# Three sums of a recurrence-and-convolution loop moved from VectorE to GpSimd, with more convolution steps in each round

## The chip, the cores and the metric

The kernel runs on one core of a Trainium2 chip. The metric is the time of one execution on the device, in microseconds. The engines are TensorE (PE: matmuls; PEld: its weight loads), VectorE (DVE), ScalarE (ACT), GpSimd (POOL) and SyncE (SP, which issues most DMAs). Each has its own queue of instructions and works through it in order; waits between engines are semaphores.

## What is computed

A two-layer backbone over 1024 latent tokens with 1024 channels and 256 context tokens. The even layer, where the change lies, projects the modulated tokens by one matrix and splits the result into five parts:

```python
va, vg, ga, xb, gb = jnp.split(z, [W_CONV, 2 * W_CONV, 3 * W_CONV, 3 * W_CONV + W_LRU], axis=-1)
y_a = conformer_conv(va, vg, p) * jax.nn.silu(ga)
y_b, hT = rglru_branch(xb, p, h0, True)
y_b = y_b * jax.nn.silu(gb)
return jnp.concatenate([y_a, y_b], axis=-1) @ p["w_out"], hT
```

`conformer_conv` gates `va * sigmoid(vg)`, runs a depthwise convolution of 31 taps along the tokens, and a layer norm over the channels. `rglru_branch` runs a short convolution of 4 taps, four gate products for each head, and a linear recurrence `h = a * h + b` along the tokens in both directions, first over the context and then over the latent tokens; `y = hs[:, :, 0] + hs[::-1, :, 1]` adds the two directions. The odd layer is a pooling mixer with two large projections; a final RMS norm ends it.

## The kernel before

**Tiling.** Channels lie on the 128 partitions, tokens along the columns. There are `KT = 8` blocks of 128 channels; a block of 1024 tokens is worked in two halves of `H = 512` columns. Every product is made of three matmuls, high part by high part, high by low and low by high (`mm3_fixed`, line 682). A weight is therefore loaded raw, its high part is cast on ACT, and its low part is the difference, by `gp` on POOL (`raw_split`, 701).

**An order written by hand.** In this part each engine's instructions are chained in the order of the program text: `on` (666) makes each instruction follow the last one of its engine. `act`, `cast`, `gp` and `vec` put instructions on ACT, ACT, POOL and DVE. So an instruction whose input is late holds up all that stands behind it on the same engine. DMAs issued by `nc.sync` are queued on SP.

**The rounds** are the loop over `j` from 903 on, one for each block of channels. Round `j` does, on PE, the products `vg` (48 matmuls), `va` (48), the context part of the next block `xbc` (24 narrow ones; not in the last round, where `gb0` takes the place of the next `xb`), and then the gate products `g` of this block, interleaved with `xb` of the next. Around them stand:

- the short convolution of block `j` on ACT and DVE (`first_tap`, `other_taps`; tile `uc`) and its split (`uh`, `ul`);
- the recurrence of block `j-1`, called `state`: `rec_input` and `rec_scaled` multiply on POOL (tiles `l`), `rec_tanh`, `rec_exp` and `rec_root` work on ACT, `rec_scan` (863) does on DVE for each direction a scaling of 1280 columns and two scans (256 and 1024 columns), and `rec_sum` (877) adds the two directions, 1024 columns, and stores the sum by SP into a DRAM buffer, `yb_raw`;
- `raw_split` of the next weights: `va`, `xb`, the gates', and in the midst of the gate products that of the next round's first weight (`vg`, or `gb` after the last round). PE reads this one at the start of the next round. On POOL it stands behind `rec_scaled`;
- the long convolution. `conv(j)` (734) is a generator of 49 steps on DVE, 50 for the last three blocks, most of them one `scalar_tensor_tensor` over some 505 columns from SBUF into an accumulator in PSUM. `fill(n)` (809) makes the next `n` steps. In rounds 1 to 7 there are 32 steps: 2 and 3 about the short convolution, 2 ahead of `ul`, 10 and 6 in `va`, 3 ahead of the context part, 6 at the end. Round 0 makes 22.

The convolution works on even and odd tokens apart (two phases) and needs, besides them, the sum of the two phases. For the first five blocks (`NSPREAD`) this sum is made ahead of its use by `spread_sum` (790) into one half of the tile `cL`; later blocks make it in a step of the convolution. `edge_sum` (786) is a product over 8 columns that goes with it. `ln_sums` (779) adds each block whose convolution has ended to two running sums, `lnsum`, one for each half, from which the layer norm's mean is made later. `at_rest` (801) calls both at the end of a round's scans, and once more after the rounds.

**The tail.** After the rounds come the products `gb1` to `gb7` and the eight of `wob` on PE. Into the stretch of `gb1` to `gb3` fall the recurrence of the last block, with `fill(2)` and `fill(24)` ahead of its `rec_scan`; then `rec_sum` and `at_rest` (1062, 1063). Then `gated` (1219) loads `yb_raw` back (tile `yr`), multiplies it on DVE by the SiLU of `gb` (tile `sb`), casts the result on ACT (`ybh`) and takes its low part on POOL (`ybl`), with a few convolution steps between; the splits of `gb5` to `gb7` and of the `wob` weights stand in the same queues. The tiles that `gated` writes lie where tiles of the rounds lay, so it waits for the last reader of those. In the `wob` products the convolutions are ended, seven steps to a half product, and the sums and the mean of the layer norm stand at a fixed place (1324).

Of the kernel before, what the change touches and what calls it, by code (L numbers as in the profile page):

```python
# [17 lines left out]
C = 256  # L18
# [3 lines left out]
H = 512  # L22
HALF = (slice(0, H), slice(H, S))
# [28 lines left out]
def body(ctx, tc, xT, ctxT, cc, ccol, modT, modW, win, gw, wout, wu, grp, wg, wo1, small, edge, ident, outT):  # L52
    nc = tc.nc
    mult, add, sub = ALU.mult, ALU.add, ALU.subtract
# [25 lines left out]
    def atile(name):  # L80
        return apool.tile([P, NR * PW], F32, tag="acc", name=name)
# [5 lines left out]
    def wide(name):  # L87
        return pc.tile([P, S], F32, tag="xb", name=name)
# [67 lines left out]
    def mm3_steps(ps, w, xs, cols, ks=KT, mm=nc.tensor.matmul):  # L156
        hi, lo = w
        xh, xl = xs
        for k in range(ks):
            kc = slice(k * P, (k + 1) * P)  # L160
            mm(ps, hi[:, kc], xh[k][:, cols], start=(k == 0), stop=False)  # L161
            mm(ps, hi[:, kc], xl[k][:, cols], start=False, stop=False)
            mm(ps, lo[:, kc], xh[k][:, cols], start=False, stop=(k == ks - 1))
            yield
# [9 lines left out]
    def col(o, n=1):  # L174
        return sm[:, o : o + n]
# [120 lines left out]
    cL = cpool.tile([P, D], F32, name="cL")  # L296
    with ExitStack() as sctx:
# [325 lines left out]
        first = (x for h in range(2) for x in mm3_steps(xb0[:, HALF[h]], ws[8], (hh, hl), HALF[h], KT, mm))  # L623
# [42 lines left out]
    def on(eng, f, *args, **kw):  # L666
        with ExitStack() as octx:
            if eng in last:
                octx.enter_context(tc.issue_after(last[eng].ins))
            last[eng] = f(*args, **kw)  # L670
        return last[eng]
# [7 lines left out]
    def gp(*args, **kw):  # L679
        return on("pool", nc.gpsimd.tensor_tensor, *args, **kw)  # L680
# [11 lines left out]
    def all_of(steps):  # L692
        for _ in steps:
            pass
# [16 lines left out]
    us = []  # L711
# [6 lines left out]
    lnacc = [atile("lnsum0"), atile("lnsum1")]  # L718
    fixed = [True]

    def vec(f, **kw):
        return on("vec", f, **kw) if fixed[0] else f(**kw)
# [53 lines left out]
    ended, summed, spread_ = [0], [1], [0]  # L776
    NSPREAD = 5

    def ln_sums():
        for j in range(summed[0], ended[0]):  # L780
            for h in range(2):
                first = us[0][:, HALF[h]] if j == 1 else lnacc[h][:, :H]
                vec(nc.vector.tensor_tensor, out=lnacc[h][:, :H], in0=first, in1=us[j][:, HALF[h]], op=add)
        summed[0] = max(summed[0], ended[0])

    def edge_sum(j):
        vec(nc.vector.scalar_tensor_tensor, out=edge_junk, in0=us[j][:, 1::2][:, H - 8 :], scalar=-1.0,
            in1=taps[:, j, 0:16:2], op0=mult, op1=mult, accum_out=edges[:, j : j + 1])

    def spread_sum():  # L790
        j = spread_[0]
        edge_sum(j)
        vec(nc.vector.tensor_tensor, out=cL[:, HALF[j % 2]], in0=us[j][:, 1::2], in1=us[j][:, 0::2], op=add)
        spread_[0] += 1

    def both_sum(j):
        while spread_[0] <= j:
            spread_sum()
        return cL[:, HALF[j % 2]]

    def at_rest():
        ln_sums()
        while spread_[0] < min(whole_[0], ended[0] + 2, NSPREAD):
            spread_sum()


    going, begun, whole_ = [iter(())], [0], [0]
# [1 line left out]
    def fill(n):  # L809
        while n > 0:  # L810
            try:
                next(going[0])
                n -= 1
            except StopIteration:
                if begun[0] >= whole_[0]:
                    return
                going[0] = conv(begun[0])
                begun[0] += 1

    with ExitStack() as actx:  # L820
# [42 lines left out]
        def rec_scan(st, d):  # L863
            at, iu = st[2][2 * d : 2 * d + 2]
            vec(nc.vector.scalar_tensor_tensor, out=iu, in0=at, scalar=1.0, in1=iu, op0=add, op1=mult)
            if d == 0:
                ctx_, lat = slice(0, C), slice(C, E)
                first = iu[:, C - 1 : C]
            else:
                ctx_, lat = slice(C - 1, None, -1), slice(E - 1, C - 1, -1)  # L870
                first = iu[:, 0:1]
            vec(nc.vector.tensor_tensor_scan, out=iu[:, ctx_], data0=at[:, ctx_], data1=iu[:, ctx_],
                initial=0.0, op0=mult, op1=add)
            vec(nc.vector.tensor_tensor_scan, out=iu[:, lat], data0=at[:, lat], data1=iu[:, lat],
                initial=first, op0=mult, op1=add)

        def rec_sum(st):
            hs, hb = st[2][1], st[2][3]
            vec(nc.vector.tensor_tensor, out=hs[:, C:], in0=hs[:, C:], in1=hb[:, C:], op=add)
            nc.sync.dma_start(yb_raw[st[0]], hs[:, C:])  # L880


# [19 lines left out]
        state, free = None, [L[0], L[1], L[2], L[3], L[4], L[5]]  # L902
        for j in range(KT):
# [66 lines left out]
            if state is None:  # L970
                for m in range(3 * KT - 2, 3 * KT):
                    gate_dot(m, gate_raw[m - 2 * KT])
                vec(nc.vector.tensor_tensor, out=m0[:, 0, 2 * KT :], in0=m0[:, 0, 2 * KT :],
                    in1=col(O_MB + 2 * KT, KT), op=add)
# [13 lines left out]
            if state is not None:  # L988
                for d in range(2):
                    rec_scan(state, d)  # L990
                rec_sum(state)
            at_rest()
            xb = wide(name if final else f"xb{j + 1}")
            steps = (x for h in range(2) for x in mm3_fixed(xb[:, HALF[h]], wnext, (hh, hl), HALF[h]))
            if state is None:
# [11 lines left out]
                    w = raw_split(raw, name)  # L1007
                    rec_input(now, 0)
            all_of(steps)
            fill(19 if state is None else 6)  # L1010
            state, uc = now, ucn


# [46 lines left out]
        gws[4] = hi, lo  # L1060
        rec_scan(state, 1)
        rec_sum(state)
        at_rest()

    cpool.release()
# [172 lines left out]
    for j in range(3, KT + 1):  # L1238
        if j == 4:
            gb_weights(j + 2)  # L1240
        if j < KT:
            gb_silu(j)
        if 4 < j < KT - 1:
            gb_weights(j + 2)
        if 3 < j < KT - 2:
            gb_product(j + 2, gws[j + 2])
        gated(j - 1, (0, 0, 4, 5, 5, 3, 1, 0)[j - 1])
        if j == KT:
            gb_weights(KT + 1)
            fill(8)  # L1250
        ln_sums()
# [62 lines left out]
    for m in range(KT):  # L1314
# [7 lines left out]
        for h in range(2):  # L1322
            all_of(steps[h])
            if (m, h) == (KT - 2, 0):
                while ended[0] < KT:
                    fill(1)
                ln_sums()
                for q, parts in enumerate([mean_parts(lnacc[q][:, :H], f"mu{q}") for q in range(2)]):
                    ln_mean(q, parts)
            elif m >= KT - 2:  # L1330
                q = m - KT + 2
                for j in range(KT) if (m, h) != (KT - 1, 1) else ():
                    ln_square(j, q)
                    if j > 1:
                        ln_add(j - 2, q)
                if (m, h) != (KT - 1, 1):
                    for j in (KT - 2, KT - 1):
                        ln_add(j, q)
                    lnparts = mean_parts(lnacc[0][:, :H], "ln0") if q == 0 else lnparts
                else:  # L1340
                    ln_root(0, lnparts)
                    lnparts = mean_parts(lnacc[1][:, :H], "ln1")
            wob_evict(m, h)
            fill(7)
            ln_sums()
# [988 lines left out]
```

## Time and profile before

| | |
|---|---|
| median of 3 runs | 1267.16 us (1267.01 to 1267.77) |
| span of the profiled execution, first to last instruction | 1263.6 us |
| what the median has beyond that span | 3.6 us |
| ACT, share of the span | 653.8 us (52%) |
| rounds 1 to 7 | 119 to 414 us from the span's start |
| gb and wob products after the rounds | 414 to 579 us |

The 3.6 us are the launch and the end, which lie outside the span; the profiled execution's own time is read as its span and these. In the lines below, `L670` is the helper `on`, so almost all instructions of this part have that one line, and they are told apart by their tiles: `l<-l,l` with 128x1280 on DVE is a scaling of the recurrence, with 128x1024 on DVE the sum of the two directions, on POOL with 128x1280 a product of the recurrence; `lnsum` is a sum for the layer norm, `cL<-u` the sum of the two phases, `wl_...` the low part of a weight. A line of a timeline gives the start and the length in us, the engine, what is written and read, how many instructions were merged (x3), and in brackets how long the engine had been idle and what ended that.

### The profile page before, as it was taken

What the parts mean: (1) busy time and instruction counts of PE and PEld (TensorE: products, weight loads), DVE (VectorE), ACT (ScalarE), POOL (GpSimd) and SP (SyncE); (2) the same over time, 40 slices, a digit from 0 to 9 for tenths busy, and PEclk for the clock granted to TensorE, in tenths of its full rate; (3) what the DMA queues carried; (4) which work ended last, traced back from release to release, by engine and by line L of the source; (5) the groups of instructions that cost most, each with busy time, mean ns of one, the idle gap of its engine ahead of it and who ended that gap; (6) DMA issues with size and microseconds to landing.
All of it is one profiled execution on the core that took longest, in us unless ns stands there. A gap on an engine that the chain in (4) does not pass through costs nothing.

```text
span 1263.6 us, 16209 instructions
## 1 busy us (share of the span) xinstructions
PE 1249.8 (99%) x5866; PEld 1035.6 (82%) x5866; DVE 1139.3 (90%) x1746; ACT 653.8 (52%) x952; POOL 295.7 (23%) x176
## 2 busy tenths in 40 slices
PE   9999999999999999999999999999999999999997
PEld 7788888888888888888887878888888888888786
DVE  7799999999999999998978969999899987977975
ACT  8464566656666534237535445744343444644642
POOL 0015364436444547543210023000000000000002
PEclk9999999999999999999999999999999999999999
DMA  9970121112121233442436666344323334759723
GB/s 376 388 254 33 52 65 46 63 43 75 42 84 42 84 119 132 159 150 84 147 112 225 202 206 183 103 136 148 125 94 140 117 125 126 268 199 335 285 71 134
DMA packets 78705, 182.29 MB, mean 144 GB/s; under 512 B 7712, under 2 KB 23328, under 8 KB 78624
## 3 DMA queue, kind: packets, MB, share of 16 engines
q1 hardware_dynamic: 67328, 172.33, 39.8%
q10 hardware_dynamic: 11296, 8.92, 2.2%
q8 instruction: 46, 0.75, 0.2%
q14 instruction: 35, 0.29, 0.1%
HBM read 137.18 MB, written 44.04 MB: 143 GB/s over the span
## 4 chain that ended last, share of the span: by engine, by line
PE 70%; DVE 18%; DMA 7%; issue 2%; ACT 2%; POOL 1%; SPq 0%; POOLq 0%; ACTq 0%; DVEq 0%
PE wob L670 7%; DVE conv L670 5%; PE va L670 5%; PE xb L670 4%; PE vg L670 4%; DVE l L670 3%; PE fold L670 3%; PE g L670 3%; PE qb_v L1153 2%; PE ga L670 2%; PE qb_g L1156 2%; PE ga L161 2%; PE qb_v L1156 2%; PE qb_g L1155 2%; PE qb_g L1153 2%
## 5 line engine op out<-in xcount | busy, mean ns | idle before, releaser
L670 DVE SCALAR_TENSOR_TENSOR conv<-u,sm,conv 128x505 f32<-128x505 f32 (+6 forms) x224 | 153.6, 744 | 1.0
L2045 POOL TENSOR_TENSOR o<-x,rr 128x256 f32<-128x256 f32 (+1 forms) x10 | 9.2, 952 | 448.4 <-ACT rr L2045 448.4
L670 ACT ACTIVATE l<-g,sm 128x512 f32<-128x512 f32 (+1 forms) x96 | 58.7, 619 | 57.7 <-PE g L670 57.0
L670 POOL TENSOR_TENSOR l<-l,l 128x1280 f32<-128x1280 f32 x16 | 47.1, 2967 | 25.6 <-ACT l L670 15.1
L670 PE MATMUL gb<-h0h,wl_gb 128*128 128x512 f32 x128 | 49.9, 390 | 0.4 <-POOL wl_gb L670 0.4
L670 PE MATMUL va<-h0h,wl_va 128*128 128x512 f32 x128 | 49.9, 390 | 0.2 <-DVE wl_va L670 0.2
L98 ACT CAST wq_g<-wr_g 128x512 fp32r<-128x512 f32 x48 | 28.2, 621 | 41.9 <-DMA wr_g<-wg 15.6
L670 PE MATMUL gb<-h0l,wh_gb 128*128 128x512 f32 x128 | 49.8, 389 | 0.0
L670 PE MATMUL gb<-h0h,wh_gb 128*128 128x512 f32 x128 | 49.8, 389 | 0.0
L670 PE MATMUL va<-h0l,wh_va 128*128 128x512 f32 x128 | 49.8, 389 | 0.0
L670 PE MATMUL va<-h0h,wh_va 128*128 128x512 f32 x128 | 49.8, 389 | 0.0
L670 PE MATMUL wob<-ybl,wh_wob 128*128 128x512 f32 x128 | 49.8, 389 | 0.0
L670 PE MATMUL wob<-ybh,wl_wob 128*128 128x512 f32 x128 | 49.8, 389 | 0.0
L670 PE MATMUL wob<-ybh,wh_wob 128*128 128x512 f32 x128 | 49.8, 389 | 0.0
L670 DVE TENSOR_TENSOR_SCAN l<-l,l 128x256 f32<-128x256 f32 (+1 forms) x32 | 48.7, 1521 | 1.1
L670 DVE SCALAR_TENSOR_TENSOR conv<-cL,wsum,conv 128x506 f32<-128x506 f32 (+3 forms) x70 | 48.1, 745 | 0.2
L670 POOL TENSOR_TENSOR l<-l,uc 128x1280 f32<-128x1280 f32 x16 | 47.6, 2999 | 0.0
L98 ACT CAST wq_wo<-wr_wo 128x512 fp32r<-128x512 f32 x48 | 28.6, 620 | 35.5 <-DVE wr_wo L1134 12.4
L98 ACT CAST wq_v<-wr_v 128x512 fp32r<-128x512 f32 x48 | 28.1, 620 | 33.7 <-DMA wr_v<-wfold 16.6
L670 PE MATMUL xb<-h0l,wh_xb 128*128 128x512 f32 x112 | 43.8, 391 | 0.0
L670 PE MATMUL xb<-h0h,wh_xb 128*128 128x512 f32 x112 | 43.8, 391 | 0.0
L670 POOL TENSOR_TENSOR wl_xb<-wr_xb,wh_xb 128x1024 fp32r<-128x1024 f32 x7 | 16.8, 2407 | 114.5 <-ACT wh_xb L670 114.5
(680 smaller groups left out, 4362.5 us busy)
## 6 DMA issues: line engine op xcount, KB each, us to landing
modw<-modW SPq DMA_DIRECT2D x16, 512.0 KB, 10.2
mod<-modT SPq DMA_DIRECT2D x32, 256.0 KB, 3.4
wr_v<-wfold SPq DMA_DIRECT2D x16, 512.0 KB, 4.0
wr_g<-wg SPq DMA_DIRECT2D x16, 512.0 KB, 4.3
wr_wo<-wo SPq DMA_DIRECT2D x16, 512.0 KB, 4.1
mod<-modT SPq DMA_DIRECT2D x14, 512.0 KB, 4.5
y_b<-y SPq DMA_DIRECT2D x24, 256.0 KB, 3.5
y_t<-y SPq DMA_DIRECT2D x24, 256.0 KB, 3.1
```

The lines of the kernel that those rows point to most:

```text
L98: return (nc.scalar.copy(hi, src), eng.tensor_tensor(out=lo, in0=src, in1=hi.bitcast(F32), op=sub))
L161: mm(ps, hi[:, kc], xh[k][:, cols], start=(k == 0), stop=False)
L670: last[eng] = f(*args, **kw)
L1153: nc.tensor.matmul(ps, hi, xh[k], start=(first and k == 0), stop=False, skip_group_check=not first)
L1155: nc.tensor.matmul(ps, hi, xl[k], start=False, stop=False, skip_group_check=not first)
L1156: mm = nc.tensor.matmul(ps, lo, xh[k], start=False, stop=(k == KH - 1), skip_group_check=not first)
L2045: tail[eng] = f(*args, **kw)
```

## The change

`ln_sums`, `spread_sum` and `rec_sum` put their additions on GpSimd through `gp` where they are called in the rounds and by `at_rest`; calls of `ln_sums` elsewhere, `both_sum`'s call of `spread_sum` and all of `edge_sum` stay on DVE. In the rounds `at_rest` now comes ahead of `rec_sum`, so that on POOL the layer norm's and the phases' sums are queued before the sum of the two directions; after the rounds the order stays as it was. The last `fill` of rounds 1 to 7 makes 10 steps instead of 6. The number of all steps stays the same, so later fills find fewer left.

```diff
+    def plus(eng, **kw):
+        (gp if eng == "pool" else lambda **k: vec(nc.vector.tensor_tensor, **k))(**kw)
+
-    def ln_sums():
+    def ln_sums(eng="vec"):
         for j in range(summed[0], ended[0]):
             for h in range(2):
                 first = us[0][:, HALF[h]] if j == 1 else lnacc[h][:, :H]
-                vec(nc.vector.tensor_tensor, out=lnacc[h][:, :H], in0=first, in1=us[j][:, HALF[h]], op=add)
+                plus(eng, out=lnacc[h][:, :H], in0=first, in1=us[j][:, HALF[h]], op=add)
         summed[0] = max(summed[0], ended[0])
...
-    def spread_sum():
+    def spread_sum(eng="vec"):
         j = spread_[0]
         edge_sum(j)
-        vec(nc.vector.tensor_tensor, out=cL[:, HALF[j % 2]], in0=us[j][:, 1::2], in1=us[j][:, 0::2], op=add)
+        plus(eng, out=cL[:, HALF[j % 2]], in0=us[j][:, 1::2], in1=us[j][:, 0::2], op=add)
         spread_[0] += 1
...
     def at_rest():
-        ln_sums()
+        ln_sums("pool")
         while spread_[0] < min(whole_[0], ended[0] + 2, NSPREAD):
-            spread_sum()
+            spread_sum("pool")
...
         def rec_sum(st):
             hs, hb = st[2][1], st[2][3]
-            vec(nc.vector.tensor_tensor, out=hs[:, C:], in0=hs[:, C:], in1=hb[:, C:], op=add)
+            gp(out=hs[:, C:], in0=hs[:, C:], in1=hb[:, C:], op=add)
             nc.sync.dma_start(yb_raw[st[0]], hs[:, C:])
...
                 for d in range(2):
                     rec_scan(state, d)
+            at_rest()
+            if state is not None:
                 rec_sum(state)
-            at_rest()
...
             all_of(steps)
-            fill(19 if state is None else 6)
+            fill(19 if state is None else 10)
             state, uc = now, ucn
```

By the program text, counted in steps, the layer norm pairs of the changed kernel fall into rounds 3, 4, 6 and 7 and into the tail (before: 3, 5, 6 and the tail), the phase sums made by `at_rest` into rounds 0 to 4 (before: 0 to 3 and 5). Between the scans of round 7 and those of the last block lie 36 steps (before: 32).

## Prediction

> **What bounds the kernel now.** I read the page's engine table first, then the chain that ended last, PE's timeline, and the table of waits on PE.
>
> ```profile
> PE 1249.8 (99%) x5866; PEld 1035.6 (82%) x5866; DVE 1139.3 (90%) x1746; ACT 653.8 (52%) x952; POOL 295.7 (23%) x176
> ```
> ```profile
> 246.64 10.88 PE vg L670 x48
> ...
> 289.12 10.88 PE vg L670 x48
> ```
> ```profile
> 331.44 0.39 PE L670 MATMUL vg<-h0h,wh_vg 128*128 128x512 f32 x1
> 331.67 0.39 PE L670 MATMUL vg<-h0l,wh_vg 128*128 128x512 f32 x1
> 331.89 0.39 PE L670 MATMUL vg<-h0h,wl_vg 128*128 128x512 f32 x1
> ```
> ```profile
> PE gb L670 <- POOL wl_gb L670: 0.4, 1, 0.4
> ```
>
> A matmul is shown as 0.39 us long, but the next one starts 0.23 us later (331.44, 331.67, 331.89): they overlap, and the distance of their starts is PE's pace. Forty-eight of them take 10.88 us in the chain, the same 0.227 us each. Round 5 begins 42.48 us after round 4 (289.12 - 246.64), and the chain between the two is all PE. So in the rounds PE never stands still: lighter work on DVE, busy as it is at 90%, shortens nothing there by itself. Between the rounds and the wob products PE waits once, 0.4 us, for a weight's low part from POOL. What the change can gain near its own place is that fraction of a microsecond; what it can lose is any new wait that reaches PE. A difference under 0.2% (2.5 us) cannot be told from no change in this kernel.
>
> **The change part by part.** DVE's rows at the end of round 5, after the scans of round 7, and in the tail:
>
> ```profile
> 314.45 1.52 DVE L670 SCALAR_TENSOR_TENSOR uc<-xbc,sm,uc 128x254 f32<-128x254 f32 x3 [0.68 <-ACT uc L670]
> 315.88 1.48 DVE L670 SCALAR_TENSOR_TENSOR l<-l,l 128x1280 f32<-128x1280 f32 x1
> ...
> 325.00 1.23 DVE L670 TENSOR_TENSOR l<-l,l 128x1024 f32<-128x1024 f32 x1
> 326.15 1.28 DVE L670 TENSOR_TENSOR lnsum<-lnsum,u 128x512 f32<-128x512 f32 x2
> 327.35 0.16 DVE L670 SCALAR_TENSOR_TENSOR edge_junk<-u,sm 128x8 f32<-128x8 f32 x1
> 327.44 0.08 DVE L670 DVE_READ_ACCUMULATOR edge_junk<-u,sm 128x1 f32 x1
> 327.44 0.69 DVE L670 TENSOR_TENSOR cL<-u 128x512 f32<-128x512 f32 x1
> ...
> 409.37 1.23 DVE L670 TENSOR_TENSOR l<-l,l 128x1024 f32<-128x1024 f32 x1
> ...
> 415.42 16.71 DVE L670 SCALAR_TENSOR_TENSOR conv<-u,sm,conv 128x505 f32<-128x505 f32 x25
> 432.04 1.48 DVE L670 SCALAR_TENSOR_TENSOR l<-l,l 128x1280 f32<-128x1280 f32 x1
> ```
>
> *On DVE.* The directions' sum takes 1.23 us in every round, a pair of layer norm sums 1.28 where a convolution has ended, the phase sum 0.69. A convolution step is 16.71/25 = 0.67 us, so four more are 2.7. A round with all three sums loses 3.2 and gets 2.7; one with the directions' sum alone gets 1.5 net. DVE's wait for ACT before the scans (0.68 in the row of 314.45) takes up part of that, so I let the scans of rounds 3 to 6 start on time. The scans of a round with their scalings are 9.1 us (315.88 to 325.00).
>
> *On POOL:*
>
> ```profile
> 266.36 5.88 POOL L670 TENSOR_TENSOR l<-l,l 128x1280 f32<-128x1280 f32 x2 [3.08 <-ACT l L670]
> 286.60 2.40 POOL L670 TENSOR_TENSOR wl_vg<-wr_vg,wh_vg 128x1024 fp32r<-128x1024 f32 x1 [14.36 <-DVE u L670]
> ...
> 393.80 5.88 POOL L670 TENSOR_TENSOR l<-l,l 128x1280 f32<-128x1280 f32 x2 [3.52 <-ACT l L670]
> 411.16 2.41 POOL L670 TENSOR_TENSOR wl_gb<-wr_gb,wh_gb 128x1024 fp32r<-128x1024 f32 x1 [11.48 <-DVE l L670]
> 413.52 5.91 POOL L670 TENSOR_TENSOR l<-l,uc 128x1280 f32<-128x1280 f32 x2
> ...
> 446.95 1.29 POOL L670 TENSOR_TENSOR ybl<-sb,ybh 128x512 fp32r<-128x512 f32 x1 [15.44 <-DMA yb_raw<-l]
> 451.35 1.78 POOL L670 TENSOR_TENSOR ybl<-sb,ybh 128x512 fp32r<-128x512 f32 x1 [3.11 <-ACT ybh L670]
> 454.82 2.41 POOL L670 TENSOR_TENSOR wl_gb<-wr_gb,wh_gb 128x1024 fp32r<-128x1024 f32 x1 [1.70 <-ACT wh_gb L670]
> ```
>
> POOL needs 1.3 us for 512 columns and 2.4 for 1024. So each layer norm sum costs 1.3 and the directions' sum 2.4. No POOL row reads every second element; I take 1.3 for the phase sum too, and keep 2.6 as its upper end. All of it lands in POOL's one long gap, 14.36 us (272.24 to 286.60 in round 4), and is queued ahead of the low part of the next round's first weight, for which PE waits next. That is the new path: scans on DVE, sum on POOL, split on POOL, PE.
>
> *Do POOL and DVE run side by side there?* Two places answer. In each, POOL's row stands first, then DVE's:
>
> ```profile
> 465.24 2.38 POOL L670 TENSOR_TENSOR wl_gb<-wr_gb,wh_gb 128x1024 fp32r<-128x1024 f32 x1
> ```
> ```profile
> 465.78 2.40 DVE L670 TENSOR_TENSOR sb<-yr,sb 128x512 f32<-128x512 f32 x1
> ```
> ```profile
> 476.24 3.59 POOL L670 TENSOR_TENSOR wl_gb<-wr_gb,wh_gb 128x1024 fp32r<-128x1024 f32 x1 [1.70 <-ACT wh_gb L670]
> ```
> ```profile
> 475.68 1.28 DVE L670 TENSOR_TENSOR lnsum<-lnsum,u 128x512 f32<-128x512 f32 x2
> 476.88 0.68 DVE L670 TENSOR_TENSOR sb<-yr,sb 128x512 f32<-128x512 f32 x1
> ```
>
> A DVE product of two SBUF tiles, 0.68 us in the last row, takes 2.40 where POOL has begun 0.54 us earlier: it ends 0.56 us after POOL's instruction. The other way round POOL's split takes 3.59 instead of 2.4 beside three such DVE instructions, as if it began only when the last had nearly ended. So they exclude each other; the 25 convolution steps of the row above, with one input in PSUM, keep 0.67 beside POOL's 5.91. The scans read two SBUF tiles. I therefore add the times of both engines up, and let DVE keep its turn through the scans, as it did through those three. [...]
>
> *Rounds 3 and 4* have the layer norm pair and the phase sum. In round 4 POOL is free at 272.24 and does one layer norm sum until 273.5; DVE scans until 282.7 and does its edge product (0.2); then POOL has 1.3 + 1.3 + 2.4 until 287.9 and the split until 290.3. PE reads that part 0.29 us into a round (331.89 less 331.60, which is 289.12 + 42.48), so at 289.4. **0.9 us lost in each**, from 0 (no exclusion) to 2.2 (phase sum at 2.6). *Rounds 1, 2 and 5* have no layer norm pair: nothing lost. *Round 6* has the pair and DVE's own product with `cL` between: **0.2**.
>
> *Round 7* has no context part, so gb1 follows sooner:
>
> ```profile
> 413.97 0.39 PE L670 MATMUL gb<-h0h,wl_gb 128*128 128x512 f32 x1
> ```
>
> POOL is free at 399.68. The pair, the scans, the sum and the split are 2.6 + 9.1 + 2.4 + 2.4 = 16.5, so the low part is there at 416.2 instead of 413.57, and PE wants it at 413.97. **2.2 us**; without exclusion 409.37 + 4.8 = 414.2, so 0.2.
>
> *The tail* carries most. Between the scans of round 7 and the last ones DVE does 36 steps instead of 32, from 409.4 on: 24.1 us. They now hold convolution 5's edge and phase sum (0.9) and its first product of two SBUF tiles, just where POOL does the input products (5.91 from 413.52): each may wait for most of one, 2.5 to 4.5 us in all; I take 3.0. The scans start at 409.4 + 24.1 + 0.9 + 3.0 = 437.4 instead of 432.0 (+5.4), the last sum takes 2.4 instead of 1.23 (+1.1), and its store goes out 6.5 us later. What hangs on it:
>
> ```profile
> 443.56 0.33 SPq L880 DMA_DIRECT2D yb_raw<-l  x1
> ```
> ```profile
> 457.50 0.40 PE L670 MATMUL gb<-h0h,wl_gb 128*128 128x512 f32 x1
> ```
>
> POOL's first `ybl` waits 15.44 us for that store to land; the next `ybl` and gb5's low part (ready at 457.23) follow in order behind it on POOL, and on SP the loads behind the store. PE takes that part at 457.50. So 457.2 + 6.5 = 463.7 against 457.5 + 2.2 (PE's own loss in round 7) = 459.7: **4.0 us**, from 0 (if the chain gives the delay back) to 7.5 (waits of 4.5, scans ending 2 later). Being later, PE has no 0.4 to wait at gb7.
>
> *After that* 28 steps fewer are left, and DVE ends its convolutions sooner, but PE's matmuls for the layer norm's mean stand at a fixed place of its order: nothing gained. Convolution 5's layer norm pair on POOL lies beside the landing of the store.
>
> Sum: 0.9 + 0.9 + 0.2 + 2.2 + 4.0 - 0.4 = **+7.8 us**. The profiled span of 1263.6 becomes 1271.4; the median of the runs is 3.6 above that span, so **1275.0 us**.
>
> **The rivals.**
>
> *Only the order counts, nothing excludes.* Rounds 3, 4 and 6 lose nothing and round 7 loses 0.2. The last scans start at 409.4 + 24.1 + 0.9 = 434.4 (+2.4), the store is 3.5 later, and gb5 gets its weight at 460.7 against 457.7: 3.0. With the 0.4 back, +2.8: 1270.0 us. Against it stand the rows at 465 and 476; for it, that all of DVE's scans in the profile ran while POOL was idle, so that they themselves were never seen to wait. Chance 0.13.
>
> *POOL's waiting adds get in between the scans.* The rounds' sums stay, since all is serial, but DVE leaves round 7's scans 2.5 us later, and the tail pays that: +10.3, 1277.5 us. For it: DVE's instructions in the scans depend on each other, so there may be short gaps; against it POOL's 3.59. [...] Chance 0.20.
>
> *Not slower.* Here DVE's load decides: the four steps vanish in waits like the 0.68, while 1.23 and 1.28 leave DVE's tail, so that the last store goes out no later than at 443.56, and PE saves its 0.4: 1266.8 us. It holds from the point where DVE reaches the last scans 1.1 us before 432.04, which pays for the slower sum. Against it: 36 steps stand where 32 did, and only one sum of 1.23 goes between these two rows. Chance 0.15, of which 0.04 is faster by over 0.2%.
>
> **How the numbers follow.** The forecast, 1273 to 1277, has 0.52; it is the likeliest. The range goes down to 1269.5 for the rival without exclusion and up to 1280 for that with adds between the scans and a dearer phase sum; "not slower" and the far ends of the tail are left out. Slower 0.85, same 0.11, faster 0.04.
>
> **What would show it.** In PE's table of waits: about 1 us for `wl_vg` in two rounds, 2 us for `wl_gb` near 414 and about 4 near 460, and none at gb7. On POOL: the sum of 1024 columns right behind DVE's scans and the split right behind the sum. If POOL's adds lie beside the scans and nothing is stretched, the exclusion is wrong; if the last scans start before 434, the tail is; if gb5's weight comes late but PE does not wait, the spare time is.

## The result and the profile after

The changed kernel takes **1276.03 us** (median of 4 runs, 1274.72 to 1278.37) against 1267.12 us before (4 runs, 1267.01 to 1267.77): the ratio, estimated from all these runs, is 1.0065, with a 95% interval from 1.0049 to 1.008. It is slower, by 8.9 us. The forecast was 1275.0 with a range from 1269.5 to 1280. The profiled execution has a span of 1272.8 us, 9.2 more than before.

The page's engine table of the changed kernel (busy us, share of the span, instructions):

```profile
PE 1252.6 (98%) x5866; PEld 1036.7 (81%) x5866; DVE 1126.9 (89%) x1724; ACT 653.7 (51%) x952; POOL 333.4 (26%) x198
```

The sums have moved: POOL has 37.7 us more and DVE 12.4 less, and PE does the same 5866 matmuls. Its table of waits, by what each waited for (us in all, times, the longest):

```profile
PE gb L670 <- ACT wh_gb L670: 3.9, 1, 3.9
PE gb L670 <- POOL wl_gb L670: 2.4, 2, 1.2
...
PE vg L670 <- POOL wl_vg L670: 0.4, 1, 0.4
```

Before, the table had one of these, `wl_gb`, with 0.4 us. Three of the new ones are the forecast's (`wl_vg`, `wl_gb` twice); the longest, for a *high* part that ACT casts, was not in it.

How much each place costs is seen better from the number of matmuls that PE gets through in a fixed stretch. First before, then after (from:to, length, then busy us and count for PE, PEld, DVE, ACT and POOL, then the granted clock of PE, the DMA share and GB/s):

```profile
276.00:300.00 24.00, 24.00 (x110) 19.95 (x110) 23.58 (x27) 13.01 (x16) 10.62 (x4) 1.00 0.16 56
396.00:420.00 24.00, 24.00 (x112) 20.00 (x111) 23.76 (x30) 16.43 (x20) 12.52 (x6) 1.00 0.12 45
450.00:480.00 30.00, 29.55 (x131) 24.14 (x130) 28.39 (x42) 12.44 (x20) 18.45 (x11) 1.00 0.32 105
```
```profile
276.00:300.00 24.00, 23.60 (x107) 19.27 (x106) 23.79 (x29) 13.01 (x16) 13.02 (x5) 1.00 0.16 55
396.00:420.00 24.00, 22.79 (x106) 18.71 (x105) 23.72 (x27) 14.56 (x19) 17.28 (x8) 1.00 0.12 45
450.00:480.00 30.00, 24.88 (x100) 19.58 (x100) 29.68 (x41) 12.41 (x20) 22.22 (x14) 0.89 0.40 132
```

A matmul of the usual size is 0.227 us of PE's pace. So 3 fewer at the end of round 4 are 0.7 us, 6 fewer at the end of round 7 are 1.4, and 31 fewer in the tail are 7.0: 9.1 of the 9.2 us. The starts of the same matmuls in both profiles say the same (0.7, 1.5 and 7.0). The last row also has a granted clock of 0.89, where the three of before have 1.00. Laid against the forecast:

| place | forecast, us | measured, us |
|---|---|---|
| round 3 | 0.9 | none seen |
| round 4 | 0.9 | 0.7 |
| round 6 | 0.2 | none seen |
| round 7 | 2.2 | 1.4 |
| tail, gb5 and gb7 together | 4.0 - 0.4 | 7.0 |
| sum | 7.8 | 9.1 |

The rounds were put too dear by 2.1 and the tail too cheap by 3.4. The two errors cancel in part, which is why the total looks better than its terms.

**Where the tail's time comes from.** The chain that ended last, in the order of time (start, length, what), from the last block's second scan of 1024 columns to PE, without the short pieces between:

```profile
448.16 2.36 DVE l L670
...
450.59 2.79 POOL l L670
...
453.39 2.83 DMA yb_raw<-l
...
456.24 4.23 DMA cH<-cc
...
461.11 1.07 ACT sb L670 x2
462.18 0.94 ACT wh_gb L670
...
463.19 2.38 POOL wl_gb L670
...
465.62 14.52 PE gb L670 x56
```

The sum of the directions on POOL is followed by its store, issued at 453.39, where it was issued at 443.56 before: 9.8 us later, not the 6.5 of the forecast. Behind it on SP stands the load of `cH`, the conditioning of the next layer. ACT's own work on that tile, a SiLU at 460.58 for which it had stood idle 6.01 us, comes ahead of the SiLU of `gb` (`sb`, 461.11) and of the cast `wh_gb` (462.07). So PE waits for the high part first, and only then for the low part that the forecast followed.

The clock belongs to the same place (the same columns as above, stretches of 2 us, changed kernel):

```profile
462.00:464.00 2.00, 0.83 (x2) 0.50 (x2) 1.97 (x4) 2.00 (x4) 0.81 (x1) 0.51 0.19 54
464.00:466.00 2.00, 0.77 (x2) 0.39 (x2) 2.00 (x3) 0.15 (x1) 2.00 (x2) 0.50 0.26 92
466.00:468.00 2.00, 2.00 (x6) 1.52 (x6) 2.00 (x5) 0.60 (x1) 2.00 (x2) 0.50 0.61 212
468.00:470.00 2.00, 2.00 (x9) 1.58 (x8) 2.00 (x5) 1.47 (x3) 0.78 (x2) 0.79 0.50 181
```

From 466 to 468 PE waits for nothing and yet has only 6 matmuls in its row of 2 us, where 9 are usual (134 in 30 us). The granted clock is 0.50, and the matmuls start 0.43 us apart instead of 0.227. From the four rows it stayed so for (0.49 + 0.50 + 0.50 + 0.21) x 2 / 0.5 = 6.8 us. In the whole stretch from 450 to 480, 34 matmuls are missing against the 134 of a full one, 7.7 us; the two waits are 3.9 + 1.2 = 5.1 of it. The other 2.6 are the clock, but for some 0.6 that such waits cost beyond their listed length (below).

**Why the store is so late.** DVE's timeline of the changed kernel: a scaling in round 4, then from the scans of round 7 to the last ones:

```profile
275.15 2.17 DVE L670 SCALAR_TENSOR_TENSOR l<-l,l 128x1280 f32<-128x1280 f32 x1
...
400.09 1.50 DVE L670 SCALAR_TENSOR_TENSOR l<-l,l 128x1280 f32<-128x1280 f32 x1
401.63 4.90 DVE L670 TENSOR_TENSOR_SCAN l<-l,l 128x256 f32<-128x256 f32 x2
...
407.95 3.08 DVE L670 TENSOR_TENSOR_SCAN l<-l,l 128x256 f32<-128x256 f32 x2
...
418.85 3.40 DVE L670 TENSOR_TENSOR u<-u 128x512 f32<-128x512 f32 x1
...
423.25 1.82 DVE L670 SCALAR_TENSOR_TENSOR conv<-u,wsum 128x512 f32<-128x512 f32 x1
...
440.28 1.48 DVE L670 SCALAR_TENSOR_TENSOR l<-l,l 128x1280 f32<-128x1280 f32 x1
```

The last scans begin at 440.28 (forecast 437.4, before 432.04). Round 7's first pair of scans takes 4.90 instead of the second pair's 3.08, so DVE leaves the scans at 411.0 and not at 409.4. Convolution 5's phase sum takes 3.40 where its like took 0.69, and its product with `wsum` 1.82. Beside these POOL was at work:

```profile
272.42 2.54 POOL L670 TENSOR_TENSOR lnsum<-lnsum,u 128x512 f32<-128x512 f32 x2
274.93 1.03 POOL L670 TENSOR_TENSOR cL<-u 128x512 f32<-128x512 f32 x1
...
285.00 2.42 POOL L670 TENSOR_TENSOR l<-l,l 128x1024 f32<-128x1024 f32 x1 [9.04 <-DVE l L670]
287.38 2.39 POOL L670 TENSOR_TENSOR wl_vg<-wr_vg,wh_vg 128x1024 fp32r<-128x1024 f32 x1
...
400.21 4.18 POOL L670 TENSOR_TENSOR lnsum<-lnsum,u 128x512 f32<-128x512 f32 x2
411.10 2.41 POOL L670 TENSOR_TENSOR l<-l,l 128x1024 f32<-128x1024 f32 x1 [6.72 <-DVE l L670]
413.47 2.39 POOL L670 TENSOR_TENSOR wl_gb<-wr_gb,wh_gb 128x1024 fp32r<-128x1024 f32 x1
415.81 5.88 POOL L670 TENSOR_TENSOR l<-l,uc 128x1280 f32<-128x1280 f32 x2
```

The pair `lnsum` at 400.21 takes 4.18 instead of 2.5 and ends at 404.4, inside the stretched scans: both engines lose. And DVE's phase sum, begun at 418.85, ends at 422.25, half a microsecond after POOL's two input products (415.81 + 5.88 = 421.69).

### The profile page after: what moved, and what is told of

It is laid out like the page before. It is cut to its first block, busy times and chain, and to the rows that moved or that the text cites. A ratio compares the mean times of both kernels' runs of the same rounds, so it can differ in the third digit from the quotient of the medians.

```text
span 1272.8 us, 16200 instructions
## 1 busy us (share of the span) xinstructions
PE 1252.6 (98%) x5866; PEld 1036.7 (81%) x5866; DVE 1126.9 (89%) x1724; ACT 653.7 (51%) x952; POOL 333.4 (26%) x198
## 4 chain that ended last, share of the span: by engine, by line
PE 64%; DVE 23%; DMA 8%; issue 3%; ACT 2%; POOL 1%; SPq 0%; POOLq 0%; ACTq 0%; DVEq 0%
DVE conv L670 9%; PE wob L670 7%; DVE l L670 4%; PE va L670 3%; PE fold L670 3%; PE gb L670 3%; PE xb L670 3%; PE vg L670 3%; PE ga L670 2%; PE ga L161 2%; PE ga L162 2%; PE ga L163 2%; DVE u L670 2%; DVE uc L670 2%; PE g L670 2%
## 5 line engine op out<-in xcount | busy, mean ns | idle before, releaser
L670 POOL TENSOR_TENSOR l<-l,l 128x1280 f32<-128x1280 f32 (+1 forms) x24 | 67.2, 2816 | 104.3 <-DVE l L670 79.3
L670 DVE TENSOR_TENSOR_SCAN l<-l,l 128x256 f32<-128x256 f32 (+1 forms) x32 | 52.1, 1627 | 1.1
L670 PE MATMUL vg<-h0h,wl_vg 128*128 128x512 f32 x112 | 43.7, 390 | 0.4 <-POOL wl_vg L670 0.4
L670 PE MATMUL vg<-h0l,wh_vg 128*128 128x512 f32 x112 | 43.6, 389 | 0.0
```

## The experiments

Two questions were put to the chip: whether the steps or the moved sums bring the loss, and through which link of the tail's chain it reaches PE. Four kernels (the sums alone, the steps alone, `fill(14)`, the last sum on VectorE) shared 23 runs of the kernel before (median 1267.27 us, 1265.45 to 1273.28), the other four 17 (median 1268.09, 1266.07 to 1269.87). Each ratio is to its own group and comes with its 95% interval; it is estimated from all the runs, so it differs a little from the quotient of the two medians.

### The sums alone

```diff
-            fill(19 if state is None else 10)
+            fill(19 if state is None else 6)
```

> The sums on GpSimd, but the last fill of a round back at 6 steps. Theory A (the loss is a chain: port shared by POOL's adds and the scans, then DVE's late arrival at the last scans, then the slower last sum): the layer norm pairs fall into rounds 3, 5, 6 as before, none into round 7, so PE waits there at most 0.3 us; DVE has 32 steps without convolution 5's products of two SBUF tiles ahead of the last scans and reaches them at about 431, as before; the last store goes out no more than 1.5 us later than at 443.6. 1267 to 1269 us. Theory B (the four steps alone are the cost, where the sums stand does not matter): the time of before or a little less, 1266 to 1267. Theory C (the slower sums on POOL alone are the cost): as with the whole change, 1275 to 1277.

1267.54 us (12 runs), ratio 0.9998 (0.9987 to 1.001). The sums on POOL with the old number of steps cost nothing that can be measured, and DVE's relief brings nothing either. Of the waits of the change PE has only one, 0.5 us for `wl_gb`, as before (0.4). Fewer steps end the convolutions later, so the layer norm's pairs fall into rounds 3, 5 and 6, as before, and none into 4 or 7, where the change waits (the pairs start at 229.91, 314.88 and 357.51 on POOL). That POOL's adds and the scans share a port, as Theory A has it, was not shown by any run; the times show only that both were longer side by side (in round 7 of the change 4.90 instead of 3.08 us for the scans, 4.18 instead of 2.5 for the pair).

### The steps alone

The kernel before with its sums on VectorE, and one edit:

```diff
-            fill(19 if state is None else 6)
+            fill(19 if state is None else 10)
```

> The four steps added per round, all sums left on VectorE as before. A: DVE gets 2.7 us a round more and its idle time is 0.7 to 2 a round, so it falls behind by some 10 us in seven rounds; PE is held by DVE's late reads of PSUM in rounds 4 to 7 and again in the tail: 1277 to 1285, more than the whole change. B: as the whole change, 1275 to 1277. C: as before, 1267.

1305.96 us (5 runs), ratio 1.0296 (1.0274 to 1.0317): 38.7 us slower. The direction was right, but the 1277 to 1285 that was expected misses the size by more than 20 us. The same stretch, 119 to 414, of the kernel before, of the sums alone and of the steps alone, in this order:

```profile
119.00:414.00 295.00, 295.00 (x1408) 248.37 (x1408) 284.55 (x365) 185.62 (x210) 142.61 (x58) 1.00 0.18 59
```
```profile
119.00:414.00 295.00, 295.00 (x1407) 248.24 (x1406) 276.07 (x351) 185.24 (x210) 176.35 (x75) 1.00 0.18 59
```
```profile
119.00:414.00 295.00, 282.46 (x1324) 235.51 (x1322) 290.64 (x357) 167.78 (x190) 138.43 (x53) 0.98 0.17 53
```

The third busy time is DVE's. Seven rounds with four steps more are 28 x 0.67 = 18.8 us. Added to the 284.55 of before they make 303.3 us of work for 295 us; added to the 276.07 of the sums alone they make 294.8, which just fits. Without the moved sums DVE no longer keeps up, and PE gets through 84 matmuls fewer (19 us). That is more than the 8 us that DVE is short of: DVE itself stands idle for 4.4 us here, and a mean granted clock of 0.98 over 295 us would stand, by estimate, for some 12 us at the 0.50 seen in the change (0.02 x 295 / 0.50). How the 19 us divide, and the further losses after 414, was not worked out. The waits on PE show how DVE's lateness arrives:

```profile
PE xbc L670 <- ACT wh_xb L670: 4.8, 1, 4.8
PE g L670 <- ACT l L670: 4.8, 3, 2.4
PE gb L670 <- ACT wh_gb L670: 3.9, 1, 3.9
```

They name ACT. For the first of them ACT is only the messenger: its cast of `uh` waited 16.98 us for DVE's `uc`, and the casts of the weights stand behind that cast:

```profile
313.83 1.26 ACT L670 CAST uh<-uc 128x1280 fp32r<-128x1280 f32 x1 [16.98 <-DVE uc L670]
```

### The change with fewer steps ahead of the last scans

In the tail 24 steps stood ahead of the last block's scans; ten of them are left for later. The number of steps between the two last groups of scans is then 26, fewer than the 32 of before.

```diff
-        fill(24)
+        fill(14)
```

> The whole change, with fill(14) in place of fill(24) ahead of the last scans (the ten steps are made later). A: DVE reaches the last scans 6.7 us sooner, at about 433.6 instead of 440.3, the last store goes out at about 446.7, gb5's weight is there before PE wants it, TensorE's clock stays at 1.00; what stays is the loss in the rounds, about 2 us: 1268 to 1270. B: the steps per round are unchanged, so 1275 to 1277. C: the sums are unchanged, so 1275 to 1277.

1267.68 us (11 runs), ratio 0.9997 (0.9987 to 1.0008): no loss can be measured any more. The last scans and the tail of this kernel, from DVE's timeline and from the stretches:

```profile
433.62 1.61 DVE L670 SCALAR_TENSOR_TENSOR l<-l,l 128x1280 f32<-128x1280 f32 x1
```
```profile
450.00:480.00 30.00, 30.00 (x134) 24.86 (x133) 29.72 (x46) 12.90 (x21) 21.73 (x13) 1.00 0.43 135
```

Scans at 433.62 instead of 440.28 and a tail at full pace, better than that of before (131). The two waits at the ends of rounds 4 and 7 are still there (0.4 and 1.2 us in its table of waits; by the starts of PE's matmuls they cost 2.2 us), and the 0.7 us that the kernel before loses at gb7 are gained. The 1.5 us that this leaves are too few to be told from nothing by these runs. So the tail is what the medians show, as the stretches said.

### Half way

```diff
-        fill(24)
+        fill(19)
```

> The whole change with fill(19) ahead of the last scans, halfway between 24 and 14. A: everything from the last scans to gb5's weight comes 3.3 us sooner than with 24, so of the 7.7 us lost there about 3 are left, without a drop of the clock if PE waits under some 3 us: 1269.5 to 1272. If what counts is only that the scans come ahead of some fixed point: the time of fill(14), 1267 to 1268.5, or of fill(24), 1275 to 1277.

1272.44 us (5 runs), ratio 1.003 (1.0018 to 1.0042), just above the 1269.5 to 1272 expected. Its profile, from one of its shorter runs (span 1268.5), has the last scans at 437.35 and this tail:

```profile
450.00:480.00 30.00, 28.18 (x124) 22.72 (x123) 29.82 (x42) 12.46 (x20) 20.34 (x13) 1.00 0.44 136
```

Ten matmuls are missing, 2.3 us, with one wait of 1.7 us for `wl_gb` and the clock at 1.00: here a wait costs 0.6 more than its listed length. Scans at 433.6, 437.35 and 440.3 lose 0, 2.3 and 7.7 us: the last 2.9 us of delay cost 5.4. More than delay is at work there.

### The last block's sum back on VectorE

`rec_sum` gets the engine as an argument; in the rounds it stays on GpSimd.

```diff
-            rec_sum(state)
+            rec_sum(state, "vec")
```

> The whole change, but the last block's sum of the two directions (after the rounds) back on VectorE. A: the last store goes out 1.5 us sooner (2.77 us on POOL against 1.23), PE's wait for gb5 shrinks by as much, and if TensorE's clock no longer drops, by up to 1.3 more: 1272.5 to 1274.5. B: 1276, no change. C: a little less than 1276, by 1.2 at most.

1275.56 us (6 runs), ratio 1.0066 (1.0044 to 1.0087): no gain clear of the noise, where 1272.5 to 1274.5 was expected. In the profile the sum takes 1.22 us on DVE instead of 2.77 on POOL, and the tail comes to

```profile
450.00:480.00 30.00, 26.17 (x108) 20.88 (x107) 29.58 (x45) 12.37 (x20) 16.78 (x11) 0.94 0.42 132
```

with 26 matmuls missing, 5.9 us instead of 7.7, so the step is worth in the tail about what the sum got shorter. In the median only 0.5 us of it is seen. Its profile loses more from 1110 to 1200 than that of the change (3.7 against 2.2 us, worked out from the starts of PE's matmuls). That stretch does not go with the tail: the sums alone and the run without the layer norm's pairs (the last one below), whose tails are at least as full as before, lose 3.0 and 2.9 there, the kernel before 1.4.

### The link through the next layer's load

The edit was meant to hold back the load of the first half of `cH`. What it moves is only ACT's SiLU of that tile, which now comes after ACT's last instruction of the gated products, so that ACT does not stand before it with the cast of `wh_gb` behind.

```diff
+    gated_last = last["act"]
...
-            load_c(0, cH, HALF[q])
+            with nullcontext() if q else tc.issue_after(gated_last.ins):
+                load_c(0, cH, HALF[q])
```

> The whole change, but the load of the conditioning vector for the next layer and its SiLU on ACT (tile cH) held back until the gated products are issued. Theory A: with the change ACT stands idle for 6.0 us in front of cH, whose load waits for the last store to land, and gb5's high part is cast only behind it; without it ACT goes on when POOL has the second ybl, so the cast comes 2.2 us sooner, PE's wait for wh_gb falls from 3.9 to about 1.7, and the clock may stay at 1.00: 1272 to 1274.5. If the store itself, not cH, sets the cast: 1276, no change.

1274.31 us (6 runs), ratio 1.0051 (1.0038 to 1.0064). The load stays where it was on SP (456.24 in the change); the start of the first half's SiLU goes from 460.6 to 503.2:

```profile
456.76 0.33 SPq L256 DMA_DIRECT2D cH<-cc  x1
```
```profile
L257 ACT ACTIVATE cH<-cH x2: 621/626/632, 503.2 to 648.0; 128x512 f32<-128x512 f32 x2
```

Its waits on PE and its tail:

```profile
PE gb L670 <- POOL wl_gb L670: 2.9, 2, 1.7
PE gb L670 <- ACT wh_gb L670: 1.6, 1, 1.6
PE qb_woa L1157 <- DVE x L1543: 1.5, 1, 1.5
```
```profile
450.00:480.00 30.00, 26.69 (x117) 21.46 (x116) 29.61 (x44) 11.96 (x19) 22.92 (x14) 1.00 0.41 132
```

The wait for the high part falls from 3.9 to 1.6, so ACT's wait for `cH` did hold up the cast. The clock stays at 1.00, with waits of 1.6 and 1.7 us; 17 matmuls are missing, 3.9 us, of which the waits are 3.3. The tail gains 3.8 us by this edit, but the median only 1.7. Part of the rest is a wait of 1.5 us in the next layer, for `qb_woa`, which was 0.5 before and is not in the table of the change. Whether that wait comes from the later SiLU was not tried; DVE first reads the tile at 618, long after 503.

### The directions' sum back on VectorE everywhere

The layer norm's and the phases' sums and the added steps stay as in the change.

```diff
-            gp(out=hs[:, C:], in0=hs[:, C:], in1=hb[:, C:], op=add)
+            vec(nc.vector.tensor_tensor, out=hs[:, C:], in0=hs[:, C:], in1=hb[:, C:], op=add)
```

> The whole change, but every sum of the two directions back on VectorE; layer norm and phase sums stay on GpSimd, ten steps stay. A: the split of the next weight no longer stands behind that sum, so the waits at the ends of rounds 4 and 7 go (-2), but DVE gets 1.2 us a round that its idle time covers only in the first rounds; it reaches the last scans 3 us later or more, and PE's clock drops again: 1274 to 1284. Theory C (the sum on POOL is the cost): 1268 to 1271.

1275.95 us (6 runs), ratio 1.0061 (1.0048 to 1.0075): no different from the change, by another way. The waits for `wl_vg` and for gb1's `wl_gb` at the ends of the rounds are gone, because the split no longer has a sum ahead of it on POOL; two of 0.35 us came in their place, from 300 to 360 (from the starts of PE's matmuls). But DVE is later: the scans of round 7 begin at 402.28 instead of 400.09, and at their end stands

```profile
412.36 3.33 DVE L670 TENSOR_TENSOR l<-l,l 128x1024 f32<-128x1024 f32 x1
```
```profile
412.21 2.40 POOL L670 TENSOR_TENSOR wl_gb<-wr_gb,wh_gb 128x1024 fp32r<-128x1024 f32 x1 [8.84 <-issue]
```

a sum of 1.23 us that takes 3.33, as POOL's split began 0.15 us ahead of it. The tail has 96 matmuls from 450 to 480, 8.6 us missing where the change has 7.7: it gives back 0.9 of the 1.4 us that the rounds gain. The last scans begin at 441.90, 1.6 us later than in the change and not the 3 that were expected.

### Without the layer norm's pairs in the rounds

The change with `fill(14)` in the tail, and the layer norm's pairs left to the `wob` products, where VectorE makes them.

```diff
     def at_rest():
-        ln_sums("pool")
...
-        fill(24)
+        fill(14)
...
-        ln_sums()
```

> The whole change with fill(14), and the layer norm pairs of the rounds and of the gated products left to the wob products, on VectorE, where it has time (same sums, same order). A: without the pairs POOL is ahead of the split in every round, so PE's waits for wl_vg and wl_gb at the ends of rounds 4 and 7 fall from 0.6 and 1.4 us to 0.3 or less, and nothing new comes: 1265.5 to 1267, not to be told from before by its time. If the sum of the directions on POOL were enough to make the split late: waits as in fill(14), 1267.7.

1266.5 us (11 runs), ratio 0.9993 (0.9984 to 1.0003). It is the lowest median of all, and not to be told from the kernel before. Its ends of round 7 and its tail:

```profile
396.00:420.00 24.00, 24.00 (x113) 20.05 (x112) 23.38 (x25) 16.16 (x20) 14.94 (x7) 1.00 0.13 45
450.00:480.00 30.00, 30.00 (x134) 24.82 (x134) 29.62 (x45) 13.50 (x23) 19.31 (x12) 1.00 0.39 127
```

Its table of waits on PE has neither `wl_vg` nor `wl_gb` nor `wh_gb`. So without the pairs the split comes in time at the ends of rounds 4 and 7. It also does without the directions' sum, in the run before this one: the waits need both in POOL's queue. And a PE that waits for none of them is worth no more against before than these runs can tell.

## Why the prediction was right, and where it was not

**Slower, since PE is at its pace and only waits can come: right.** No version with the moved sums or the steps was measurably faster than before, the best is the one without a new wait.

**Steps and sums.** The forecast let the scans of rounds 3 to 6 start on time, because the sums leave DVE nearly what the steps bring. The steps alone show what that cover was worth: 38.7 us without it. The sums alone lose nothing. But "on time" held for round 3 only (230.78 against 230.93 before); the scans of round 4 began 0.9 us later than before, of round 5 2.0, of round 6 0.4.

**Rounds 3, 4, 6 and 7: the path right, what delays it wrong in part, the term too large** (4.2 against 2.1). The path of scans, sum, split and PE is what the profile shows: POOL's sum begins at 285.00, just after the scans, and its split behind it. What comes ahead of that sum was wrong. The forecast ends round 4's scans at 282.7, but in the profile of before they begin at

```profile
274.28 1.48 DVE L670 SCALAR_TENSOR_TENSOR l<-l,l 128x1280 f32<-128x1280 f32 x1
```

and so end at 283.4; with that row its own sum gives 1.6 us for round 4 instead of 0.9. It also kept POOL's waiting adds out until the scans had ended, and took 1.3 us for the phase sum, which took 1.03. In fact both layer norm sums of round 4 and its phase sum were done by 275.96, beside DVE's last products that read PSUM, which kept their times (2.04 and 1.51 us, 2.05 and 1.52 before). Round 4 was late because its scans began 0.9 us later and their first scaling was held up by POOL, 2.17 instead of 1.48 us. In round 7 POOL's pair got in beside the first scans, which took 4.90 instead of 3.08. This is the rival "POOL's waiting adds get in between the scans". It was right that they do, and came near its price in the scans (DVE leaves them 1.6 us later, it said 2.5), but not about the rounds, which it left at their full price. Round 7 was also cheaper because PE came to it 0.7 us late already, from round 4, while the scans began at 400.09, no later than the 400.24 of before. The forecast added up the losses of the rounds as if each began anew; a PE that is late already has less to wait for the next weight.

**The tail: the right place, the term too small** (3.6 against 7.0). Three things in it. The store goes out 9.8 us later instead of 6.5. Of the 3.3 between them round 7's scans are 1.6; the three operations of convolution 5 lost 4.0 instead of 3.0, inside the stated 2.5 to 4.5 (0.42, 3.40 and 1.82 against 0.16, 0.69 and 0.76), which is 1.0; and the last sum on POOL took 2.77 instead of 2.4, which is 0.4; the other 0.3 was not traced. The chain that PE waits for was not the one followed: the forecast went from the store over POOL's `ybl` to the low part; the chain of waits goes over SP to the load of `cH`, over ACT, to the high part, and the run with ACT's work on `cH` put off shows that this link is real. And the clock was not thought of at all; it is about 2 us of the 7 (below).

**Not slower, and only the order counts: wrong.** The last scans began at 440.28, far from the 430.9 that the first needed; against the second, round 7's first scans took 4.90 us instead of 3.08 beside POOL's pair, and the pair 4.18 instead of 2.5.

**After that, nothing gained: not contradicted.** The losses named make up the whole difference of the spans but 0.1 us. By the starts of PE's matmuls the change gains 0.7 us between 720 and 750 against before and loses 0.9 between 1110 and 1200; the sums alone do the same (0.8 and 1.6) without a loss in the tail, so neither is put down to the change.

**The 3.6 us beyond the span: near by luck.** They were carried over from the kernel before as launch and end. But the profiled execution of the change took 1274.72 us with a span of 1272.8, so only 1.9 us lie outside it. Most of the rest of the 3.6 must be that the one profiled execution of before was shorter than its median. For the change the same difference is 3.2, because its profiled execution, too, was one of the shorter.

**Left open.** Why the shorter tails of two runs (the last sum on VectorE, the later SiLU of `cH`) appear only in part in their medians. And what sets the loss from 1110 to 1200, which differs from profile to profile.

## What to carry to other kernels

Here PE ran at its pace, and moving additions to an engine that was busy 23% of the span bought nothing by itself (1267.54 us against 1267.27); ask what stands behind each addition in its new queue, and whether the next weight is among it. Filling the time won on the old engine with work from elsewhere cost nothing that could be measured only where what was added between two links of a serial chain was taken out at another place (ten steps ahead of the last scans, 1267.68 us); without that the last scans began 8.2 us later than before (440.28 against 432.04), and the time was 1276.03. A wait on one engine is best followed back over every queue that it crosses; the engine that the table names may only pass it on, as ACT did here with the 3.9 us for `wh_gb`, which led over its 6.01 us of idling for `cH` back to a store on SP.

## What the hardware showed beside that

*The clock.* In the change the granted clock of PE fell to 0.50 just after 462, during the wait of 3.9 us and some 3 us after the last matmul ahead of it had begun (458.89), and stayed there for 6.8 us, over the wait of 1.2. With the last sum on VectorE the waits were 2.1 and 1.8 us, and the clock was 0.50 for 3.4 us from 464.1; with waits of 1.6 and 1.7 us (the later SiLU of `cH`) it stayed at 1.00. So a drop does not need a single wait of 3 us, as the forecast for `fill(19)` had supposed. The drop explains, with the longer waits (5.1 us instead of 1.7), why the last 2.9 us of delay cost 5.4. No run here tells from which length of a wait the clock drops, or whether two waits count together.

*POOL's addition of every second element.* The changed kernel's four phase sums on POOL (shortest, median and longest in ns); they lie in rounds 1 to 4, and the first block's is made on DVE at 101.8:

```profile
L670 POOL TENSOR_TENSOR cL<-u x4: 1032/1060/1423, 144.6 to 274.9; 128x512 f32<-128x512 f32 x4
```

At the median, 1.06 us, it is shorter than the 1.29 us of the shortest of POOL's layer norm sums in this profile, over as many contiguous columns. The dearer end of the forecast, 2.6 us, was far off.
